# A two-layer streaming encoder step: attention, its entry and the kernel's end reworked together, and the engines' instruction order taken from a time line

## The chip, the cores and the metric

The kernel runs on one core of a Trainium2 chip. TensorE (PE in the profile) multiplies matrices, VectorE (DVE) and ScalarE (ACT) do elementwise work, GpSimd (POOL) does a little more of it, and SyncE (SP) issues most of the transfers. The metric is the device time of one execution in microseconds (us), taken as the median over several runs; lower is better.

## The reference

One step of a hybrid encoder over 1024 prompt rows and 64 sample rows (1088 columns in all, here stored transposed, features on the partitions). Layer 0 is a state-space mixer with a convolution, layer 1 a banded attention; a SwiGLU feed-forward network (FFN) follows each, and every sub-layer is wrapped in two RMSNorms.

```python
def rmsnorm(x, w):
    y = xf * lax.rsqrt(jnp.mean(xf * xf, axis=-1, keepdims=True) + EPS)
    return (y * w.astype(jnp.float32)).astype(x.dtype)

def swiglu(u, w_in, w_out):
    g, up = jnp.split(u @ w_in, 2, axis=-1)
    return (jax.nn.silu(g) * up) @ w_out

def shared_kv(x, kv_norm_w, w_kv):
    kv = (rmsnorm(x, kv_norm_w) @ w_kv).reshape(b, L, 2, ATT_HEADS, ATT_HEAD_DIM)

def band_attend(q, k, v, qpos, kpos, rel_bias):
    ...
    s = jnp.einsum('bqhd,bkhd->bhqk', q, k).astype(jnp.float32) * (ATT_HEAD_DIM ** -0.5) + bias
    s = jnp.where(valid, s, -jnp.inf)
    p = jax.nn.softmax(s, axis=-1).astype(v.dtype)
    return jnp.einsum('bhqk,bkhd->bqhd', p, v)
...
    xp = xp + rmsnorm(mp, nw[1])
    xp = xp + rmsnorm(swiglu(rmsnorm(xp, nw[2]), ffn_w_in[layer], ffn_w_out[layer]), nw[3])
```

Each query sees its own 64-row chunk and the eight before it. There are 16 heads of 64; the kernel handles them as 8 pairs `j`.

## The kernel before, in words

**Precision.** Every large product is made of three: a weight tile and an activation are each split into a rounded high part and a remainder, and `passes` (L407) multiplies high by high, high by low and low by high (L415 to L417). So every weight block of 128x1024 that arrives by DMA in a tile `raw` costs ACT a copy (L312, the high part `hl`) and DVE a subtraction (L313, the low part).

**Weights.** `Weights` is a planner with a fixed order: `plan` lists the blocks, `load` issues their DMAs, `plain` (L242) splits them. Blocks of the key, value and query projections carry a scale by row (`kscale`, the norm's weight): POOL multiplies the block by it in place first (L248), and then the split follows. `W.pri` gives the split a priority, `W.eng` another engine for the subtraction (POOL for the first three blocks).

**Order.** The columns come in three slices `s` of 384, 384 and 320. PE's order is written out by hand: the program issues PE's instructions exactly in program order, and a small clock `st.t` decides where the side tasks (`st.spawn`, `yield cost, delay, condition`) are put between the units of a projection. The constants `EP_W`, `ER_W`, `EQ_W`, `AT_W1` and so on are delays of that clock. The other engines' orders and the order of the DMA issues on SP are chosen when the program is built, by a list scheduler which follows program order shifted by `tc.high_priority(n)` (n instructions earlier).

**Stages.** Mixer (to about 660 us), its output projection and the first FFN (to about 1650), attention (to about 2200), its output projection and the second FFN (to the end). In the mixer `Conv` (L710) turns a projection's result into a tile `raw`, filters it into a tile `cvt` of which there is one, and applies Silu into the destination.

**The FFN's second half** (`back`, from L1388 on): for each slice eight output tiles, 66 matmuls each; `end(s)` then normalizes the slice, adds the residual and, in layer 0, splits the sum as the attention's input `u[s]` and forms the next norm's sum of squares. `rb_steps` (L482) is the norm's chain: `rstd` (matmuls with a column of ones, L448, then eight small DVE operations), a diagonal matrix `dg` on DVE (L467), one matmul that spreads it (L475) and an ACT copy to `rb`.

**Attention.** For each pair `j` and slice `s` the units K, Q and V are projected in that order; `evk`, `evq`, `evv` scale each result by `rba[s]` and split it. Q's low part is written twice, on both halves of the partitions, by DVE (L1540). `v_task` transposes V. `att_task(j, b)` handles a block of 128 query rows for both heads of the pair in three steps whose order is kept by `cur`: A, the scores (L1610, L1611) into one of two PSUM tiles `S` and the softmax on DVE and ACT (L1617 to L1626); B, the transposes of the probabilities into the same PSUM ring (`ptp`, L1638) and their copies `pT` (L1642); C, the product with V (L1661), after each block. At the entry the units of slice 2 are issued only once slice 2's norm is done; `build_o` reads the attention's result back from DRAM for the output projection.

Of the kernel before, what the change touches and what calls it, by code (L numbers as in the profile page):

```python
# [16 lines left out]
P = 128  # L17
# [31 lines left out]
EP_W, ER_W, EQ_W = (9.4, 9.4, 5.0), (8.9, 8.9, 4.5), (11.0, 11.0, 11.0)  # L49
# [4 lines left out]
LDP, ENP = 1500, (0, 0, 1500)  # L54
# [8 lines left out]
NB0 = 5  # L63

NACC = 3
BIG = 1e30
# [134 lines left out]
class Weights:  # L201
# [40 lines left out]
    def plain(self, it):  # L242
# [3 lines left out]
        if it.get("kscale") is not None:  # L246
            v3 = r.rearrange("p (k m) -> p k m", m=P)
            self.nc.gpsimd.tensor_tensor(v3, v3, it["kscale"].unsqueeze(2).to_broadcast([P, KD, P]), op=ALU.mult)  # L248
        self.part(it, "w", None, r[:, :n])
# [85 lines left out]
def hybrid_kernel(  # L335
# [4 lines left out]
    nc = tc.nc  # L340
    V, A, G, PE = nc.vector, nc.scalar, nc.gpsimd, nc.tensor
# [101 lines left out]
    def rstd(ssum, inv, r, nb, more=None):  # L443

        sp, ts = ax("nst"), [ssum] if more is None else [ssum, more]
        for i in range(nb):
            for j, t in enumerate(ts):
                PE.matmul(  # L448
                    sp[:, i:i + 1], t[:, i * P:(i + 1) * P], ones[:, 0:1], start=(j == 0), stop=(j == len(ts) - 1)
                )  # L450
        with tc.high_priority(HIP):
            v = nsb.tile([P, 12], F32, tag="nv", bufs=2, name="nv")
            a, h, y = v[:, 0:nb], v[:, 4:4 + nb], v[:, 8:8 + nb]
            V.tensor_scalar(a, sp[:, :nb], inv, EPS, op0=ALU.mult, op1=ALU.add)
            V.tensor_scalar(y.bitcast(I32), a.bitcast(I32), -0.5, float(0x5F3759DF), op0=ALU.mult, op1=ALU.add)
# [145 lines left out]
    with ExitStack() as es:  # L601
# [108 lines left out]
        class Conv:  # L710
# [5 lines left out]
            def __call__(self, s, ps_):  # L716
# [19 lines left out]
                cvt = sb2.tile([P, 384], F32, tag="cvt", bufs=1, name="cvt")  # L736
                cw = C_CW + ct * 4
                A.activation(cvt[:, :w_], raw[:, 0:w_], AF.Identity, bias=col(C_CB + ct), scale=col(cw))
                for k in range(1, 4):
                    V.scalar_tensor_tensor(  # L740
                        cvt[:, :w_], raw[:, k:k + w_], col(cw + k), cvt[:, :w_], op0=ALU.mult, op1=ALU.add
                    )
                if s < 2:
                    A.activation(dst[:, :384], cvt[:, :384], AF.Silu)
                else:
                    A.activation(dst[:, 0:256], cvt[:, :256], AF.Silu)  # L746
                    A.activation(dst[:, 256:320], cvt[:, 259:323], AF.Silu)
# [244 lines left out]
        W.eng = G  # L992
# [16 lines left out]
        for s in range(NSL):  # L1009
# [11 lines left out]
            for i in range(3):  # L1021
# [7 lines left out]
                if s == 2 and i == 2:  # L1029
                    W.eng = None  # L1030
# [245 lines left out]
    def back(layer, start, cpost, xsrc, xmid, cpre, cpost2, xout, rb_out, done2):  # L1276
# [3 lines left out]
        with ExitStack() as es:  # L1280
# [21 lines left out]
            def end_load(s):  # L1302
                o, n = SL[s]
                xc = Cells(n, (R, 99)) if s == 2 else Cells(n, (RX, 99), (R, 99))
                yield 0, EP_W[s], lambda: xc.room(KD)
# [5 lines left out]
            def end(s, y, ss, more=None):  # L1311
# [6 lines left out]
                yield from rb_steps(ss, n, out, ER_W[s], more=more)  # L1318
# [140 lines left out]
    for j in range(1, 8):  # L1459
        W.plan(W_K[j], W_Q[j], W_V[j])  # L1460
# [408 lines left out]
```

## Time and profile before

| what | us |
| --- | --- |
| median of 3 runs (lowest, highest) | 3090.92 (3090.6, 3097.8) |
| the profiled execution's own time | 3083.24 |
| its span, first to last instruction | 3081.1 |
| PE busy | 2989.6 |
| DVE busy | 2117.1 |
| ACT busy | 1419.9 |
| POOL busy | 880.4 |

The profile follows one execution. A row of a group gives engine, line, operation, written tile and read tiles, count and mean duration; a row of the timeline gives start and duration and, in brackets, how long the engine stood idle before it and which instruction ended that. "Granted clock" is the share of TensorE's full clock in a stretch. The profiled execution was 7.7 us faster than the median of the runs.

### The profile page before, as it was taken

How to read it: one execution, taken by the hardware profiler on the slowest of the kernel's cores; microseconds unless marked ns; L12 is line 12 of the kernel's file. 1: busy time of each engine (PE TensorE's matmuls, PEld its weight loads, DVE VectorE, ACT ScalarE, POOL GpSimd, SP SyncE). 2: the span in 40 equal slices, each digit the busy share in tenths (PEclk: the TensorE clock that was granted, in tenths of full speed). 3: DMA queues.
4: the chain of work that ended last, by engine and by line, in shares of the span. 5: the costliest groups of instructions: out<-in, count | busy, mean ns of one | idle time of the engine just before them, and what ended most of it. 6: DMA issues, size and time to landing. Idle time of an engine off the chain costs nothing.

```text
span 3081.1 us, 56781 instructions
## 1 busy us (share of the span) xinstructions
PE 2989.6 (97%) x21761; PEld 2908.2 (94%) x21761; DVE 2117.1 (69%) x4579; ACT 1419.9 (46%) x2512; POOL 880.4 (29%) x1011
## 2 busy tenths in 40 slices
PE   8999999999999999999999899999999999999998
PEld 8899999999999999999999788889898999999997
DVE  8878788796778545574566788887768645575544
ACT  6656565664443222344443454444554332244432
POOL 2333333331344343341223111100054334342112
PEclk9999999999999999999999999999999999999999
DMA  3111111125553222345663121122355222246654
GB/s 118 39 52 51 57 51 59 51 89 151 170 166 107 83 78 74 99 149 176 194 188 123 61 68 60 55 61 62 114 168 166 78 78 76 79 124 183 205 181 132
DMA packets 176511, 329.14 MB, mean 107 GB/s; under 512 B 17360, under 2 KB 124752, under 8 KB 176240
## 3 DMA queue, kind: packets, MB, share of 16 engines
q1 hardware_dynamic: 174448, 319.16, 33.4%
q0 software_dynamic: 1792, 6.36, 1.1%
q8 instruction: 171, 2.80, 0.4%
q14 instruction: 100, 0.82, 0.1%
HBM read 262.85 MB, written 62.60 MB: 106 GB/s over the span
## 4 chain that ended last, share of the span: by engine, by line
PE 81%; DVE 10%; DMA 3%; issue 2%; ACT 2%; POOL 2%; SPq 0%; DVEq 0%; POOLq 0%; ACTq 0%
PE mm L415 8%; PE px L1235 8%; PE px L1236 8%; PE px L1237 8%; PE mm L417 8%; PE mm L416 8%; PE po L1407 5%; PE po L1405 5%; PE po L1406 5%; PE mmx L415 2%; PE mmx L416 2%; PE mmx L417 2%; PE po L1661 2%; PE ptp L1638 2%; DVE hl L313 1%
## 5 line engine op out<-in xcount | busy, mean ns | idle before, releaser
L313 DVE TENSOR_TENSOR hl<-raw,hl 128x1024 fp32r<-128x1024 f32 (+1 forms) x292 | 359.7, 1233 | 313.5 <-ACT hl L312 312.9
L415 PE MATMUL mm<-r,hl 128*128 128x384 f32 (+2 forms) x1664 | 560.3, 337 | 5.9 <-ACT BT L746 4.8
L417 PE MATMUL mm<-r,hl 128*128 128x384 f32 (+2 forms) x1664 | 540.2, 325 | 0.6 <-DVE hl L313 0.6
L416 PE MATMUL mm<-r,hl 128*128 128x384 f32 (+2 forms) x1664 | 539.8, 324 | 0.0
L312 ACT CAST hl<-raw 128x1024 fp32r<-128x1024 f32 (+1 forms) x295 | 297.8, 1014 | 302.1 <-PE po L1407 98.7
L1236 PE MATMUL px<-r,hl 128*128 128x288 f32 (+1 forms) x1192 | 350.1, 294 | 0.0
L415 PEld LDWEIGHTS mm<-r,hl 128*128 128x128 f32 x1664 | 316.2, 190 | 14.6 <-issue 6.7
L441 POOL TENSOR_TENSOR ssum<-ssum,sq 128x256 f32<-128x256 f32 (+3 forms) x153 | 166.0, 1091 | 540.8 <-ACT sq L440 537.6
L416 PEld LDWEIGHTS mm<-r,hl 128*128 128x128 f32 x1664 | 316.5, 190 | 0.4
L417 PEld LDWEIGHTS mm<-r,hl 128*128 128x128 f32 x1664 | 315.6, 190 | 1.0 <-DVE hl L313 1.0
L1235 PE MATMUL px<-r,hl 128*128 128x288 f32 x1056 | 311.7, 295 | 4.1 <-DVE u L1250 3.9
L1237 PE MATMUL px<-r,hl 128*128 128x288 f32 x1056 | 311.2, 295 | 0.0
L1237 PE MATMUL px<-rx,hl 128*128 128x256 f32 x816 | 229.1, 281 | 6.5 <-DVE hl L313 6.5
L1235 PE MATMUL px<-rx,hl 128*128 128x256 f32 x816 | 230.0, 282 | 0.0
L1236 PEld LDWEIGHTS px<-r,hl 128*128 128x128 f32 x1192 | 224.0, 188 | 0.1
L1406 PE MATMUL po<-rx,hl 128*128 128x384 f32 (+1 forms) x640 | 208.0, 325 | 0.0
L1235 PEld LDWEIGHTS px<-r,hl 128*128 128x128 f32 x1056 | 198.7, 188 | 5.7 <-DVE u L1250 5.7
L1405 PE MATMUL po<-rx,hl 128*128 128x384 f32 (+1 forms) x608 | 199.6, 328 | 0.0
L1237 PEld LDWEIGHTS px<-r,hl 128*128 128x128 f32 x1056 | 198.4, 188 | 0.0
L1407 PE MATMUL po<-rx,hl 128*128 128x384 f32 (+1 forms) x608 | 198.0, 326 | 0.3 <-DVE hl L313 0.3
L1236 PE MATMUL px<-rx,hl 128*128 128x256 f32 x680 | 191.1, 281 | 0.0
L262 POOL TENSOR_TENSOR tt<-raw 128x512 f32<-128x512 f32 x44 | 60.0, 1363 | 396.9 <-DMA raw<-in_w_f_dram 207.8
(348 smaller groups left out, 8147.4 us busy)
## 6 DMA issues: line engine op xcount, KB each, us to landing
raw<-in_w_f_dram SPq DMA_DIRECT2D x204, 512.0 KB, 3.8
raw<-in_w_in_dram SPq DMA_DIRECT2D x40, 512.0 KB, 3.6
raw<-in_w_f_dram SPq DMA_DIRECT2D x48, 384.0 KB, 3.2
sg<-hscr SPq DMA_DIRECT2D x88, 192.0 KB, 3.6
raw<-in_w_so_dram SPq DMA_DIRECT2D x32, 512.0 KB, 3.9
raw<-in_w_kv_dram SPq DMA_DIRECT2D x18, 512.0 KB, 3.6
raw<-in_w_o_dram SPq DMA_DIRECT2D x16, 512.0 KB, 3.8
sg<-hscr SPq DMA_DIRECT2D x44, 160.0 KB, 3.6
```

Source lines behind the costliest of these rows:

```text
L312: self.nc.scalar.copy(h, v)
L313: (eng or self.eng or self.nc.vector).tensor_tensor(lo, v, h, op=ALU.subtract)
L415: PE.matmul(ps[:, :n], h_, xh, start=(first and i == 0), stop=False)
L416: PE.matmul(ps[:, :n], h_, xl, start=False, stop=False)
L417: PE.matmul(ps[:, :n], l_, xh, start=False, stop=(last and i == nk - 1))
L441: (eng or G).tensor_tensor(ssum[:, :n], ssum[:, :n], q[:, :n], op=ALU.add)
L1235: PE.matmul(ps, wh, ah[:, k, :], start=(k == 0), stop=False)
L1236: PE.matmul(ps, wh, al[:, k, :], start=False, stop=False)
L1237: PE.matmul(ps, wl, ah[:, k, :], start=False, stop=(k == 3))
L1405: PE.matmul(ps[:, :n], wh, xh, start=(k == 0), stop=False)
L1406: PE.matmul(ps[:, :n], wh, xl, start=False, stop=False)
L1407: PE.matmul(ps[:, :n], wl, xh, start=False, stop=(k == FT - 1))
```

## The change

- **Scheduler.** The whole kernel is traced in a second, inner context inside a critical section, with `schedule_with_timeline_sim=True`: the orders of DVE, ACT, POOL and SP come from another simulated machine. PE's order stays that of the program.
- **Weights with a row scale.** POOL's multiplication is gone; `scaled` makes the high part by eight ACT operations of 128x128 with a scale and the low part by eight DVE operations.
- **Mixer.** The convolution filters in place in its destination (`cvt` is gone); the first three weight blocks are subtracted by DVE, not POOL.
- **FFN's second half.** Weight splits get priority 1500 (`W.pri = LDP`). The end of slice 2 starts earlier (2.2 and 3.3 on the clock for 5.0 and 4.5), and its additions are all on DVE.
- **Entry.** Slice 2's K and V units of pair 0 are issued before slice 2's norm is done, and only their scaling waits for it; V of pair 1 for slices 0 and 1 comes before slice 2's Q.
- **Attention.** Order K, V, Q; score tasks are spawned by Q. The maximum's two small DVE operations go (the reduction runs on negated values and chains its start value). The second half of Q's low part is copied by a DMA on SP. Step C of a slice's three blocks is issued together, before step B of the next slice's first block. Scales at priority 3000, softmax and `pT` copies at 1000. Three tiles of Q become two, four of `pT` six. The last pair's result is taken from SBUF by `build_o`.
- **Kernel's end.** The last norm's two partial sums are summed in separate columns; six of the eight residual additions are made by PE (an identity times the residual, added in PSUM to an identity times the scaled result) and copied out by ACT.

```diff
-EP_W, ER_W, EQ_W = (9.4, 9.4, 5.0), (8.9, 8.9, 4.5), (11.0, 11.0, 11.0)
+EP_W, ER_W, EQ_W = (9.4, 9.4, 2.2), (8.9, 8.9, 3.3), (11.0, 11.0)
...
         if it.get("kscale") is not None:
-            v3 = r.rearrange("p (k m) -> p k m", m=P)
-            self.nc.gpsimd.tensor_tensor(v3, v3, it["kscale"].unsqueeze(2).to_broadcast([P, KD, P]), op=ALU.mult)
-        self.part(it, "w", None, r[:, :n])
+            self.scaled(it, r)
+        else:
+            self.part(it, "w", None, r[:, :n])
...
+    def scaled(self, it, r):
+
+        self.used.append(self.hl)
+        t = self.hl.get()
+        for k in range(KD):
+            sl, c = slice(k * P, (k + 1) * P), it["kscale"][:, k:k + 1]
+            self.nc.scalar.activation(t[:, 0, sl], r[:, sl], AF.Copy, scale=c)
+        for k in range(KD):
+            sl, c = slice(k * P, (k + 1) * P), it["kscale"][:, k:k + 1]
+            self.nc.vector.scalar_tensor_tensor(t[:, 1, sl], r[:, sl], c, t[:, 0, sl], op0=ALU.mult, op1=ALU.subtract)
+        it["w"] = t[:, 0, :], t[:, 1, :]
...
+    ctx.enter_context(tc.tile_critical())
+    tc = ctx.enter_context(tile.TileContext(nc, schedule_with_timeline_sim=True))
...
-        W.eng = G
...
             def end(s, y, ss, more=None):
...
+                    yield next(steps)
+                    hold(range(4))
+                    yield next(steps)
+                    yield next(steps)
+                    hold((4, 5))
+                    for m in range(KD):
+                        ym = y[:, m, :n]
+                        V.scalar_tensor_tensor(ym, ym, col(cpost2 + m), out[0], op0=ALU.mult, op1=ALU.mult)
+                        if m in xps:
+                            PE.matmul(xps[m][:, :n], ident, ym, start=False, stop=True)
+                            A.copy(ym, xps[m][:, :n])
+                        else:
+                            V.tensor_tensor(ym, ym, xs[m][0], op=ALU.add)
+                        nc.sync.dma_start(xout[:, m, o:o + n], ym)
...
-                yield 0, EQ_W[s]
+                yield (0, EQ_W[s]) if s < 2 else (0, 0, lambda: "k2" in done2)
...
             phase[0] = 2
+
+            W.pri = LDP
...
-                    for x in range(2):
-                        V.tensor_tensor(ql[H2[x], :n], qf[H2[e], :n], qh[H2[e], :n], op=ALU.subtract)
+                    V.tensor_tensor(ql[H2[e], :n], qf[H2[e], :n], qh[H2[e], :n], op=ALU.subtract)
+                    nc.sync.dma_start(ql[H2[1 - e], :n].bitcast(F32), ql[H2[e], :n].bitcast(F32))
+                for i in range(3):
+                    st.spawn(att_task(j, 3 * s + i), 5.0 + 0.1 * i)
...
-                if split < w_:
-                    V.tensor_tensor(mx[:L, 0:1], mx[:L, 0:1], mx[:L, 1:2], op=ALU.max)
-                V.tensor_scalar(mx[:L, 2:3], mx[:L, 0:1], -1.0, None, op0=ALU.mult)
-                A.activation(sc[:L, :w_], sc[:L, :w_], AF.Exp, bias=mx[:L, 2:3], accum_out=mx[:L, 3:4])
...
+                low = TOP
+                with tc.high_priority(ATP):
+                    for pi, (f0, f1) in enumerate([(0, split)] + ([(split, w_)] if split < w_ else [])):
+                        V.tensor_tensor_reduce(
+                            out=sc[:L, f0:f1], in0=sp[:L, pi, :f1 - f0], in1=brev[:, f0:f1],
+                            scale=-1.0, scalar=low, op0=ALU.add, op1=ALU.min, accum_out=mx[:L, pi:pi + 1],
+                        )
+                        low = mx[:L, pi:pi + 1]
...
+            cost = values(held) if i == 0 else 0
...
-        st.wait_for(lambda: ("rb", 2) in done)
...
-        for w, e in ((wk, evk), (wq, evq), (None, evv)):
-            units(w or W.get(), 0, e, (2,))
+        wv = W.get()
+        n2, kv2 = SL[2][1], []
+        for w in (wk, wv):
+            ps = mm("mm")
+            passes(ps, w, lambda k: u[2][k], [(k, k) for k in range(KD)], n2, parts=4)
+            kv2.append(ps)
+            done.append("k2")
+            st.pump()
+        st.wait_for(lambda: ("rb", 2) in done)
+        for ps, e in zip(kv2, (evk, evv)):
+            e(0)(2, ps)
             W.put()
+            st.pump()
```

More of the change, by code (lines that the diff above doesn't have):

```diff
@@ L1317, in end, with hold @@
                 out = []
-                yield from rb_steps(ss, n, out, ER_W[s], more=more)
+                if s == 2 and more is None:
+                    yield 0, EP_W[2]
+                steps = rb_steps(ss, n, out, ER_W[s], more=more)
+                if more is not None:
+                    xps = {}
+                    def hold(ms):
+                        for m in ms:
+                            xps[m] = mm("xp") if m > 3 else px.tile([P, 512], F32, tag="mm", name="xp")
+                            PE.matmul(xps[m][:, :n], ident, xs[m][0], start=True, stop=False)
+                    yield next(steps)
[12 more added lines that the diff above has]
+                        nc.sync.dma_start(xout[:, m, o:o + n], ym)
+                    for c in xs:
+                        xc.put(c)
+                    yr.put()
+                    return
+                yield from steps
                 for m in range(KD):
```

211 lines of the change are left out of this document (117 added, 94 removed).

## The prediction, made before the result was known

> **What bounds the kernel now.** The page first: how much of the span PE is busy, and who stands in the chain that ended last.
>
> ```profile
> span 3081.1 us, 56781 instructions
> PE 2989.6 (97%) x21761; PEld 2908.2 (94%) x21761; DVE 2117.1 (69%) x4579; ACT 1419.9 (46%) x2512; POOL 880.4 (29%) x1011
> PE 81%; DVE 10%; DMA 3%; issue 2%; ACT 2%; POOL 2%; SPq 0%; DVEq 0%; POOLq 0%; ACTq 0%
> ```
>
> PE is the bound, and the change takes no matmul away. All it can win is PE's idle time (3081.1 − 2989.6 = 91.5 us) and the slow clock behind a stall. So the next view is the busy time by stretches, cut at the stages that the change touches (stretch, length, then PE, PEld, DVE, ACT, POOL busy; granted clock).
>
> ```profile
> core 0: us, PE busy (x) PEld busy (x) DVE busy (x) ACT busy (x) POOL busy (x), PEclk, DMA share, GB/s
> 0.00:160.00 160.00, 144.77 (x933) 134.17 (x934) 132.44 (x327) 102.87 (x176) 44.69 (x96) 0.98 0.24 80
> 160.00:660.00 500.00, 499.35 (x3484) 484.54 (x3483) 399.75 (x1036) 305.36 (x478) 165.30 (x313) 1.00 0.17 54
> 660.00:1590.00 930.00, 919.43 (x6802) 911.48 (x6802) 590.63 (x1016) 380.58 (x663) 298.00 (x263) 1.00 0.44 134
> 1590.00:1610.00 20.00, 16.48 (x92) 15.95 (x91) 16.09 (x15) 10.28 (x19) 12.86 (x11) 0.83 0.64 201
> 1610.00:1670.00 60.00, 60.00 (x387) 59.54 (x387) 30.96 (x52) 22.43 (x37) 19.34 (x14) 1.00 0.42 129
> 1670.00:1700.00 30.00, 23.64 (x131) 22.83 (x130) 23.84 (x56) 13.49 (x29) 6.77 (x11) 0.83 0.36 118
> 1700.00:1800.00 100.00, 89.34 (x675) 80.15 (x674) 81.74 (x257) 48.51 (x110) 13.99 (x11) 0.97 0.19 58
> 1800.00:2200.00 400.00, 383.53 (x2984) 353.60 (x2984) 320.11 (x997) 195.32 (x434) 29.68 (x35) 1.00 0.21 63
> 2200.00:3000.00 800.00, 787.12 (x5849) 782.00 (x5848) 482.12 (x777) 318.77 (x538) 273.87 (x247) 0.99 0.45 135
> 3064.00:3081.10 17.10, 2.96 (x15) 1.85 (x14) 10.05 (x23) 0.86 (x2) 2.99 (x3) 0.60 0.22 77
> ```
>
> Idle on PE is length minus busy: 3.5 us at 1590, 6.4 at the entry (1670), 10.7 and 16.5 in attention, 14.1 at the end; 0.65 in 500 us of mixer, where nothing can be won and DVE is 80% busy. These five places are the ones that the change addresses.
>
> **The change part by part.**
>
> *Weights first in the FFN's second half.* PE's timeline around the stall, with two rows of the matmuls behind it:
>
> ```profile
> 1602.18 0.42 PE L1405 MATMUL po<-r,hl 128*128 128x320 f32 x1 [2.50 <-ACT hl L312]
> 1603.76 0.64 PE L1407 MATMUL po<-r,hl 128*128 128x320 f32 x1 [1.02 <-DVE hl L313]
> 1604.46 0.47 PE L1406 MATMUL po<-rx,hl 128*128 128x320 f32 x1
> 1609.53 0.47 PE L1407 MATMUL po<-rx,hl 128*128 128x320 f32 x1
> ```
>
> The weight's split stood behind the end of slice 1 on ACT and DVE. Between the last two rows 19 matmuls start, 0.267 us apart, where the stretch after has 60/387 = 0.155 on average: 20 x 0.11 = 2.2 us more. At priority 1500 against 0 the split goes first. Late next are slice 1's additions, by two splits (some 2.3 us), with 60 us until attention reads them. At most −5.7; I take −5. At the other end 0, if the block itself lands late.
>
> *Entry.*
>
> ```profile
> 1676.29 0.58 PE L448 MATMUL nst<-ones,ssum 128*128 128x1 f32 x2 [3.95 <-POOL ssum L1352]
> 1679.29 2.29 PE L448 MATMUL nst<-ones,ssum 128*128 128x1 f32 x10 [2.41 <-DVE ssum L1352]
> ```
>
> PE has only the norm of slice 2 left and waits 6.4 us for its sums. Now two units of 24 matmuls each (48 x 0.155 = 7.4 us) need no norm, the first ahead of these rows and the second between them and `nbp`; the end of slice 2 also starts 2.8 + 1.2 clock units earlier, and its eight additions no longer share the time with POOL (four more on DVE, about 2 us). Left is the wait from `rb` to the first free PSUM bank, about 1 us (copy and scale). I take −6; ends −7.4 and +4 (if the sums are as late as now and Q, moved behind V of pair 1, delays the first scores by that).
>
> *Attention.* First who PE waits for between 1690 and 2200, then the event that recurs once a pair: POOL's scaling of a weight block, DVE's Q remainders and PE's wait.
>
> ```profile
> PE ptp L1638 <- DVE mx L1617: 12.1, 7, 2.6
> PE S L1610 <- ACT pT L1642: 9.2, 10, 1.2
> L1540 DVE TENSOR_TENSOR Ql<-qf,Qh x52: 461/552/2228, 1847.7 to 2119.0; 64x384 fp32r<-64x384 f32 x32, 64x320 fp32r<-64x320 f32 x20
> 1848.66 3.10 DVE L1540 TENSOR_TENSOR Ql<-qf,Qh 64x320 fp32r<-64x320 f32 x3
> 1849.42 1.99 POOL L248 TENSOR_TENSOR raw<-raw,pcs 128x1024 f32<-128x1024 f32 x1 [2.04 <-DMA raw<-in_w_kv_dram]
> 1852.74 1.66 PE L1638 MATMUL ptp<-ident,sc 128*128 128x128 f32 x10 [1.47 <-DVE mx L1617]
> ```
>
> The two rows of waits hold 21.3 of the 27.2 us idle between 1700 and 2200: PSUM tiles that DVE or ACT had not emptied. At 1848.66 three remainders take 3.10 us where three of the shortest to the median (0.46 to 0.55) take 1.5: POOL runs from 1849.42 beside the last. Behind them the reductions come late, and the transposes wait for the tile until 1852.74.
>
> What DVE saves by pair: from 1850 to 2050 there are three pairs (48 negations on 128 partitions, 16 a pair: eight blocks of two heads), so a pair is about 67 us.
>
> ```profile
> L313 DVE TENSOR_TENSOR hl<-raw,hl 128x1024 fp32r<-128x1024 f32 x9 | 11.0, 1222 | 1.7 <-ACT hl L312 1.6
> L1623 DVE TENSOR_SCALAR mx<-mx 128x1 f32<-128x1 f32 x48 | 6.7, 150 | 0.5
> L1622 DVE TENSOR_TENSOR mx<-mx 128x1 f32<-128x1 f32 x24 | 3.7, 156 | 0.2
> 23.40 0.29 DVE L990 TENSOR_TENSOR dtw<-dtr,dtw 128x128 fp32r<-128x128 f32 x1
> 22.38 0.50 ACT L989 CAST dtw<-dtr 128x128 fp32r<-128x128 f32 x2
> L312 ACT CAST hl<-raw 128x1024 fp32r<-128x1024 f32 x9 | 9.4, 1048 | 11.3 <-issue 9.2 <-PE mm L417 1.9
> ```
>
> Half of twelve remainders (6 x 0.55 = 3.3), the negation and maximum ((6.7 + 3.7)/3 = 3.5) and one blocked stretch (1.6) go: 8.4 us of 320.11/6 = 53.4. Eight operations of 128x128 at most 8 x 0.29 = 2.3 replace a subtraction of about 1.2: 1.1 a block, 3.3 for three. Net −5 on DVE; ACT gets 8 x 0.25 − 1.05 = 1 more per block, with half its time free. POOL loses 1.99 a block and stands ahead of no split any more. Higher priority on softmax and `pT` empties PSUM sooner. What stays: V's products of three blocks now stand in one piece, and a slice's first transposes stand behind them.
> I take −16, some 0.6 of the idle time. Ends: −27, and +23 for one wait as the row of 1.47 at each of 24 slices less the 12.1 gone.
>
> *Q's remainder by DMA.* Not shown before; the nearest transfers of its size:
>
> ```profile
> out_kT_dram<-kf SPq DMA_DIRECT2D x3, 128.0 KB, 1.7
> SPq L1669 <- ACT ot L1668: 105.8, 22, 18.3
> ```
>
> So 1.7 us (64 x 384 x 4 = 96 KB), against 0.55 on DVE, and behind whatever SP's queue waits for: `ot` was waited for up to 18.3 us. Cover: Q is projected one slice (a third of a pair, 22 us) ahead of its scores. I take 0; uncovered it costs 1.7 − 0.55 = 1.2 for each of 24 slices, 28 us.
>
> *End.*
>
> ```profile
> 3068.16 1.43 PE L475 MATMUL nbp<-dg,frac 128*128 128x320 f32 x2 [2.23 <-DVE dg L467]
> 1659.85 0.70 PE L475 MATMUL nbp<-dg,frac 128*128 128x320 f32 x2
> 3070.09 4.30 DVE L1326 SCALAR_TENSOR_TENSOR y<-y,pcs,rb 128x320 f32<-128x320 f32 x5 [1.98 <-ACT rb L479]
> 3075.24 2.08 DVE L1327 TENSOR_TENSOR y<-y,r 128x320 f32<-128x320 f32 x5
> 3077.25 0.54 DVE L1324 SCALAR_TENSOR_TENSOR y<-y,pcs,r 128x320 f32<-128x320 f32 x1
> ```
>
> From `rb` to the end of DVE's last, 3077.8, is 7.7 us; the scalings take 4.30/5 = 0.86 each while POOL works on three of the eight. After: eight at 0.54 and two additions at 2.08/5 = 0.42, 5.2 in all. PE's last six identities at 0.70 (4.2) and ACT's copies run beside. The four held ones (2.8) fill the 2.23 idle ahead of `nbp` and 0.6 more; `nbp` then takes 0.70 for 1.43. So −2.5 + 0.6 − 0.7 = −2.6. Cold, at 1.43 each, the four would take 5.7 (+3.5 ahead of `nbp`) and the six 8.6, 0.9 over the 7.7 of now, and a last copy of 0.4: about +5. The Trainium skill ("TensorE: Matmul & The Clock Gate", section "What's actually happening") says that the clock halves after an idle window of about 3.4 us and is whole again after as long a busy one. By that rule a tail of short bursts could stay cold, and the sum would be 7.6 worse; the pair 1.43 and 0.70 agrees with the halving, though the idle time before it was 2.23 only.
>
> *The rest.* The in-place filter and three subtractions moved from POOL to DVE: 0, between −3.6 and +3.6 (3 x 1.2 on a DVE that is 83% busy in the first 160 us). Entering and leaving an inner context: +1, between 0 and 2.1 (what lies around the span now, 3083.24 − 3081.1, once more). A new order for four engines everywhere else: 0; it can win at most the idle of the untouched stretches (15.2 + 0.65 + 10.6 + 12.9 = 39), and its loss is a rival.
>
> Sum: −5 − 6 − 16 − 2.6 + 1 = −28.6, so 3054.6 for an execution like the profiled one. That one was 7.7 under the median; on the median's scale 3090.9 − 28.6 = 3062.
>
> **The rivals.** 0.3% (9 us) is about what a measurement can tell from no change here.
>
> *The gain is eaten in attention.* Q's DMA is uncovered (28 us), because SP's queue holds it or Q comes late; or the merged products make PE wait as often as now. Against it the 22 us of lead. From 17 slices on (17 x 1.2 = 20) what is left is under 9 us. Time 3091 − 29 + 28 = 3090.
>
> *Slower: the new order costs the mixer.* PE has no idle time there only because order and hand-written delays fit.
>
> ```profile
> L821 ACT ACT_TABLE_LOAD x38 | 48.8, 1283 | 32.7 <-DVE dm L817 32.4
> ```
>
> Of 160 to 660 us this is one place of loads; Exp and Silu alternate in each step, and every further split of an Exp pair adds 1.283 us to the chain from `bcp` to the product. With 48 steps (16 pairs of heads by 3 slices), one load more on each: 48 x 1.283 = 62 us, so 3062 + 62 = 3124. It decides from 23 uncovered loads on (29/1.283). For it: DVE at 80%; against: ACT has 39% of the stretch free, and each of its 38 steps has 500/38 = 13 us. The Trainium skill ("ScalarE: Activation LUTs", "What ACT_TABLE_LOAD costs") gives 2.66 us for a switch with its drain; by that estimate it would be 128 us, but the row shows 1.283 and no drain.
>
> *The tail stays cold:* −28.6 + 7.6 = −21, 3070; for it the 1.43 of now, against it that the held identities leave no gap. *The order helps everywhere:* half of the 39 us besides: about 3042.
>
> **How the numbers follow.** Forecast 0.55, of which 0.12 with a cold tail (own range 3045 to 3078); helps everywhere 0.06, eaten 0.12, slower 0.27. So faster 0.61, same 0.12, slower 0.27. The range goes from 3036 to 3116: it leaves out some 0.03 below and the worse half of the slower case, 0.15, above.
>
> **What would show it.** No wait over 1 us at the second FFN slice's weights near 1600; PE busy through the entry; waits of `ptp` on the reduction down from 12.1 to under 4 in all, and Q remainders of 0.5 only; the tail after the last FFN matmul at 14 us for 17. Mixer idle above 10 us, or more than 38 table loads at the line of the Exp there, would make it wrong.

## The result and the profile after

The changed kernel takes 3110.68 us (3104.76 to 3114.58) against 3090.92 us of the kernel before: a ratio of 1.0057, 95% interval 1.0041 to 1.0072. It is slower, by about 18 us (20 between the medians), where 29 us faster was forecast. It lies inside the range (3036 to 3116), in the case that had 0.27.

The page of the changed kernel, its span and its busy times:

```profile
span 3109.1 us, 57030 instructions
PE 3000.5 (97%) x21785; PEld 2927.8 (94%) x21785; DVE 2066.3 (66%) x4498; ACT 1455.8 (47%) x2701; POOL 817.7 (26%) x975
```

DVE has 51 us less to do (2117.1 before) and POOL 63 us less, as the change says. PE has more of both: 108.6 us idle for 91.5, and 3000.5 us busy for 2989.6 with only 24 matmuls added. PE's waits (what it waited for, us in all, times, longest) say where:

```profile
PE nbp L490 <- DVE dg L482: 13.1, 6, 4.0
PE po L1445 <- DVE hl L313: 12.8, 10, 2.6
PE nst L463 <- POOL ssum L455: 10.3, 5, 3.8
...
PE px L1247 <- DVE p L1264: 5.9, 2, 3.1
...
PE ptp L1688 <- DVE mx L1666: 2.2, 3, 1.1
```

The wait that led the list before, of the transposes for the reduction (12.1 us), is down to 2.2. New at the top are waits for the norm's chain (`dg`, the diagonal matrix, and `ssum`, its sums), for the sums `p` of the FFN's first half, and for weight splits. Two rows of the kernel before for the same work: `dg` 2.2 us once, and 2.3 us in all for the splits of the FFN's second half:

```profile
PE po L1407 <- DVE hl L313: 2.3, 4, 1.0
PE nbp L475 <- DVE dg L467: 2.2, 1, 2.2
```

Three of these waits on PE's timeline of the changed kernel, with what follows the third:

```profile
825.72 1.19 PE L490 MATMUL nbp<-dg,frac 128*128 128x256 f32 x2 [3.02 <-DVE dg L482]
...
998.63 0.39 PE L1247 MATMUL px<-rx,half 128*128 128x256 f32 x1 [3.09 <-DVE p L1264]
...
1641.01 0.60 PE L1445 MATMUL po<-rx,hl 128*128 128x320 f32 x1 [2.54 <-DVE hl L313]
1641.41 0.47 PE L1443 MATMUL po<-rx,hl 128*128 128x320 f32 x1
...
1644.35 0.38 PE L1445 MATMUL po<-rx,hl 128*128 128x320 f32 x1
1644.57 0.31 PE L1443 MATMUL po<-rx,hl 128*128 128x320 f32 x1
```

A wait is paid more than once: for 3.3 us behind the third the matmuls take 0.47 us each for 0.31, and start 0.267 us apart for 0.147 later. Twelve of them cost 12 x 0.12 = 1.4 us on top of the 2.54. So waits make PE's busy time grow too. The same 21785 matmuls in the list order (`e2_rework_inner_plain`, below) keep PE busy for 2985.1 us, at a mean granted clock of 0.992 for 0.985 here:

```profile
PE 2985.1 (98%) x21785; PEld 2915.1 (95%) x21785; DVE 2074.0 (68%) x4498; ACT 1461.0 (48%) x2703; POOL 814.9 (27%) x975
```

The Trainium skill ("TensorE: Matmul & The Clock Gate", section "What's actually happening") has the clock halve after an idle window of about 3.4 us and recover after as long a busy one; the 3.3 us agree, but here 2.54 us of waiting were enough.

### The profile page after: what moved, and what is told of

It reads as the page before. It is cut to its first block, busy times and chain, and to the rows that moved or that the text cites. A ratio compares the mean times of both kernels' runs of the same rounds, so it can differ in the third digit from the quotient of the medians.

```text
span 3109.1 us, 57030 instructions
## 1 busy us (share of the span) xinstructions
PE 3000.5 (97%) x21785; PEld 2927.8 (94%) x21785; DVE 2066.3 (66%) x4498; ACT 1455.8 (47%) x2701; POOL 817.7 (26%) x975
## 5 line engine op out<-in xcount | busy, mean ns | idle before, releaser
L313 DVE TENSOR_TENSOR hl<-raw,hl 128x1024 fp32r<-128x1024 f32 (+1 forms) x269 | 321.7, 1197 | 305.3 <-ACT hl L312 303.5
L312 ACT CAST hl<-raw 128x1024 fp32r<-128x1024 f32 (+1 forms) x269 | 271.5, 1010 | 290.1 <-DMA raw<-in_w_f_dram 120.6
```

What stands on the lines that cost most here:

```text
L312: self.nc.scalar.copy(h, v)
L313: (eng or self.eng or self.nc.vector).tensor_tensor(lo, v, h, op=ALU.subtract)
```

## The experiments

### The three parts apart: the rework, the inner context, the time line

The change holds three things: the rework of the kernel, an inner context in a critical section, and in it the order from the time line. Two runs take parts off the changed kernel.

`e1_rework_plain_order`: the rework alone, in the outer context.

```diff
-    ctx.enter_context(tc.tile_critical())
-    tc = ctx.enter_context(tile.TileContext(nc, schedule_with_timeline_sim=True))
+
+
```

> The changed kernel without the inner context and its time line: the rework alone, the engines' order chosen as in the kernel before. Theory A (the order costs the time, the rework wins it): the forecast's sum holds, 3091 - 30 = 3061 us, faster by 0.7 to 1.2%; the first FFN's pairs begin at about 952 us as before (981 in the changed kernel), the last score at about 2177. Theory B (the rework itself costs outside attention: in-place filter, subtractions on DVE, weight splits first): the start of the pairs stays at about 980 and the time at 3105 to 3115. Theory C (both by halves): about 3085.

`e2_rework_inner_plain`: the inner context stays, the order is that of the list scheduler.

```diff
-    tc = ctx.enter_context(tile.TileContext(nc, schedule_with_timeline_sim=True))
+    tc = ctx.enter_context(tile.TileContext(nc, schedule_with_timeline_sim=False))
```

> The changed kernel with the inner context kept and the time line switched off. Theory A with the time line as the cause: within 3 us of the run without an inner context, 3061 to 3065 (the context costs one entry and one exit, 0 to 2 us). Rival: the inner context itself is what changes the order for the worse; then about 3110 as in the changed kernel.

`e3_before_time_line` and `e4_before_inner_plain`: the kernel before with the same two lines added, with `True` and with `False`.

> The kernel before with the inner context and the time line, and nothing else of the change. Theory A: it pays what the order costs without what the rework wins, 3091 + 48 = 3139 (3125 to 3150), with the pairs of the first FFN starting near 981. Theory B: the order is harmless, 3085 to 3095, pairs near 952.

> The kernel before in an inner context without the time line. Theory A: 3091 to 3094, the cost of entry and exit alone. Rival (the inner context disturbs the order): over 3100, and then the time line's own part is the difference to the run of the kernel before with the time line.

Measured, as ratios to the kernel before (3087.0 us on that chip), with 95% intervals:

| order | kernel before | rework |
| --- | --- | --- |
| outer context, list order | 1 | 0.9849 (0.9832 to 0.9866), 3038.6 us |
| inner context, list order | 1.0049 (1.0032 to 1.0065), 3101.0 us | 0.9919 (0.9902 to 0.9935), 3060.7 us |
| inner context, time line | 1.0184 (1.0164 to 1.0205), 3140.9 us | 1.0057 (1.0041 to 1.0072), the change |

So the rework alone is worth 1.5%, some 47 us, more than the 29 forecast for everything. The inner context costs 15 us on one kernel and 22 on the other (0.0049 and 0.0070 of 3087). The time line's order costs 42 and 43 us (0.0135 and 0.0138): the same on both, so it is no matter of the rework. A difference of two ratios, here and below, is uncertain by some 7 us either way (two intervals of 0.0017).

Against what was expected: the rework alone is on the side of Theory A (the pairs of the first FFN start at 958.2 us, not at 980), but 22 us faster than its figure of 3061. `e2` meets its 3061 to 3065 almost to the microsecond, and by luck: its condition, within 3 us of the run without the inner context, fails by 19. `e3` is Theory A (3140.9 for 3139, the pairs at 979.8). `e4` lies above 3100, as its rival had it, but not for the rival's reason: its trace has every engine's instructions in the same order as in the kernel before.

PE's hand-written order and its delays were the same in all of these runs. Whether another order on PE would suit the time line's orders better was not run.

Where each part acts can be read from landmarks, the starts of the same work in each profile (us; from the views of one tile's instructions, which give the first and last start of each group):

| | before | + inner | + time line | rework | + inner | + time line |
| --- | --- | --- | --- | --- | --- | --- |
| first transposes of the mixer | 91.4 | 96.0 | 91.2 | 98.2 | 102.6 | 89.3 |
| last transposes of the mixer | 657.4 | 663.1 | 663.3 | 664.1 | 669.1 | 663.8 |
| FFN 1, first half, first matmul | 951.8 | 960.1 | 979.8 | 958.2 | 965.7 | 980.5 |
| FFN 1, second half, first matmul | 1372.5 | 1382.1 | 1408.0 | 1378.6 | 1388.7 | 1406.8 |
| attention, first scores | 1694.0 | 1704.6 | 1740.5 | 1686.9 | 1700.7 | 1723.1 |
| attention, last scores | 2206.1 | 2215.6 | 2245.7 | 2167.2 | 2184.1 | 2220.5 |
| FFN 2, second half, last matmul | 3063.8 | 3078.1 | 3127.3 | 3023.3 | 3042.5 | 3093.2 |
| end | 3081.1 | 3097.7 | 3146.4 | 3037.0 | 3058.4 | 3109.1 |

The last column less the one before it: the time line wins 13 us at the start, has given back 8 of them by the end of the mixer, is 15 us behind at the first FFN, 22 at the first scores, 36 at the last, and 51 at the end. So the largest losses are the 20 us between the mixer and the first FFN (its output projection and the norms), 14 in attention and 14 behind it; the long first half of the first FFN loses only 3. (The columns are of one execution each. The 51 us at the end, where the ratios give 43, are of executions in different rounds, in which the kernel before took 3090.9 and 3087.0 us.)

PE's order is the same in these two kernels and every engine has the same instructions (but for 2 of ACT's 100 table loads), so what differs is the order on the other engines and what comes late for it. DVE's timeline in the changed kernel, ahead of two of the waits shown above:

```profile
820.22 0.16 DVE L478 SCALAR_TENSOR_TENSOR nr<-nv 128x2 f32<-128x2 f32 x1
820.29 0.46 DVE L577 TENSOR_TENSOR r<-sg,r 128x288 fp32r<-128x288 f32 x1
820.66 3.03 DVE L1180 SCALAR_TENSOR_TENSOR rx<-rx,pcs,rb 128x256 f32<-128x256 f32 x5
823.61 0.45 DVE L577 TENSOR_TENSOR r<-sg,r 128x288 fp32r<-128x288 f32 x1
823.98 1.26 DVE L1180 SCALAR_TENSOR_TENSOR rx<-rx,pcs,rb 128x256 f32<-128x256 f32 x3
825.16 0.41 DVE L482 TENSOR_TENSOR dg<-ident,nr 128x256 f32<-128x256 f32 x1
...
993.43 0.41 DVE L1262 TENSOR_TENSOR u<-px,p 128x256 f32<-128x256 f32 x1
993.76 3.88 DVE L1122 TENSOR_TENSOR r<-r 128x1152 fp32r<-128x1152 f32 x3
997.57 0.68 DVE L281 TENSOR_TENSOR tt<-raw,tt 128x512 f32<-128x512 f32 x1
998.17 0.41 DVE L1264 TENSOR_TENSOR p<-px,p 128x256 f32<-128x256 f32 x1
```

And the same two places with the list order (`e2_rework_inner_plain`):

```profile
816.68 0.15 DVE L478 SCALAR_TENSOR_TENSOR nr<-nv 128x2 f32<-128x2 f32 x1
816.76 0.46 DVE L577 TENSOR_TENSOR r<-sg,r 128x288 fp32r<-128x288 f32 x1
817.13 0.42 DVE L482 TENSOR_TENSOR dg<-ident,nr 128x256 f32<-128x256 f32 x1
...
976.00 0.41 DVE L1262 TENSOR_TENSOR u<-px,p 128x256 f32<-128x256 f32 x1
976.33 1.68 DVE L280 TENSOR_TENSOR tt<-tt,raw 128x512 f32<-128x512 f32 x1
977.93 1.35 DVE L1122 TENSOR_TENSOR r<-r 128x1152 fp32r<-128x1152 f32 x1
979.20 0.41 DVE L1264 TENSOR_TENSOR p<-px,p 128x256 f32<-128x256 f32 x1
```

The diagonal matrix needs `nr` and nothing else. In the list order it starts 0.5 us behind `nr`; in the time line's, eight scalings and two subtractions stand between, and it is 4.9 us. At the second place 4.6 us of work that has time stand ahead of `p`, for 3.0 in the list order. There `u`, just ahead, was late as well: PE waits 1.88 us for it at 993.9. In these rows DVE works in the order that it was given, so an urgent operation that is put behind a long one waits, however ready it is.

### Is an urgent chain that loses its place enough?

The rows show it, but no run so far made that change alone. `e13_chains_without_priority` does, in the plain order: the priority 3000 is taken from the norm's chain, its diagonal matrix, its copy to `rb`, and from the sums of the FFN's first half, `u` and `p` among them.

```diff
-        with tc.high_priority(HIP):
+        with tc.high_priority(0):
             v = nsb.tile([P, 12], F32, tag="nv", bufs=2, name="nv")
...
-        with tc.high_priority(HIP):
+        with tc.high_priority(0):
             dg = diag(nr[:, :nb], nb)
...
-        with tc.high_priority(HIP):
+        with tc.high_priority(0):
             out.append(bcast(dg, 0, n, rb))
...
-            with tc.high_priority(HIP):
+            with tc.high_priority(0):
                 if p_ == P1:
```

> The rework in the plain order, with the priority 3000 taken from the norm's chain (the small operations, the diagonal matrix, the copy to rb) and from the sums u and p, and nothing else changed. Between the rework's inner plain order and its time line, with the same instructions and the same order on PE, PE's waits for the diagonal matrix go from under 1 to 13.1 us and for p from under 1 to 5.9 us, and 43 us are lost. Theory A, an urgent chain that other DVE work gets into is enough to lose time: 10 to 30 us slower than the rework in the plain order, ratio 0.988 to 0.995, with waits for the diagonal matrix and for u and p of 2 to 4 us each at several norms. Theory B, the waits named are only where delays from elsewhere (late weights, late transfers) show: ratio 0.984 to 0.987, and these waits stay as they were.

Ratio 0.9982 (0.9972 to 0.9991), 3080.3 us: 41 us slower than the rework in the plain order, more than Theory A gave. PE's waits in it, and one of them with what stands ahead of it on DVE:

```profile
PE px L1247 <- DVE u L1262: 17.5, 4, 8.8
PE nbp L490 <- DVE dg L482: 13.5, 5, 5.7
```

```profile
987.00 6.42 DVE L1122 TENSOR_TENSOR r<-r 128x1152 fp32r<-128x1152 f32 x5
993.34 0.41 DVE L1262 TENSOR_TENSOR u<-px,p 128x256 f32<-128x256 f32 x1
```

```profile
993.81 0.58 PE L1247 MATMUL px<-rx,hl 128*128 128x256 f32 x1 [7.85 <-DVE u L1262]
```

The waits stand at the same places as in the changed kernel (at 830, 994, 1724, 2299 and 2394 us here; 826, 994 and 999, 1739, 2309 and 2413 there). So losing the place of these chains is enough to lose as much as the time line loses. It isn't shown that it is all of it, and PE's waits say that it is about half. Here PE idles 28.6 us more than in the plain order, and 27 of them are waits for these chains. In the changed kernel PE idles 35 us more than in `e2` (108.6 for 73.3), and these chains have some 18 of them; weight splits of the FFN's second half have 8.4, sums on POOL 6.5, and the inputs of the mixer's transposes 6.4. No run takes these others away.

### What the inner context costs

The list order inside and outside of the inner context is the same, instruction by instruction and wait by wait, but for a few branches and barriers at both ends. The difference of 22 us is in how long things take. SyncE's timeline of the rework in the outer and then in the inner context (start, duration of the issue):

```profile
1101.00 0.33 SPq L224 DMA_DIRECT2D raw<-in_w_f_dram  x1
```

```profile
1101.58 0.50 SPq L224 DMA_DIRECT2D raw<-in_w_f_dram  x1
```

and the median from issue to landing of the same transfers, in the same order:

```profile
raw<-in_w_f_dram SPq DMA_DIRECT2D x204, 512.0 KB, 3.6
```

```profile
raw<-in_w_f_dram SPq DMA_DIRECT2D x204, 512.0 KB, 4.0
```

Each issue takes 0.17 us longer (0.33 and 0.50 are the medians of all 1119 issues on SyncE too), and these transfers land 0.4 us later; the kernel before shows the same (0.33 and 3.8 against 0.50 and 4.0). Everything that goes through a transfer is a little later; PE's waits for `u` rise from 4.8 to 6.6 us, and the granted clock of the first 100 us falls from 0.93 to 0.90. The time is not lost evenly but in steps: the same matmul starts 4.9 us later at any point of the mixer from 205 to 664 us, 8.0 later from 1031 to 1280 in the first half of the first FFN, and 17.9 from 2434 to 2684 in that of the second. So a stream of matmuls that waits for nothing runs as fast as before. Of the 21.4 us between the two spans (3037.0 and 3058.4) 9.7 are idle time of PE, and 11.7 are busy time at a lower granted clock (0.995 and 0.992). No run changes the issues alone, so that they are the whole cause is argued, not shown.

`e8_small_section_first` asks whether it is enough to stand behind such a section:

```diff
+    with tc.tile_critical(), tile.TileContext(nc) as tn, tn.tile_pool(name="first", bufs=1) as fp:
+        nc.vector.memset(fp.tile([P, 4], F32, name="first"), 0.0)
```

> The rework in the plain order, with a critical section and an inner context ahead of it that hold one small memset; the kernel itself stays in the outer context, and each engine's order is that of the plain one. The rework wholly inside an inner context has the same instructions in the same order, and yet its DMA issues take 0.45 to 0.50 us on SP for 0.33, its transfers land 0.2 to 0.4 us later, and it is 22 us slower. Theory A, it is enough that the code stands behind the section's branch: issues of 0.45 to 0.50 and ratio 0.990 to 0.993. Theory B, it takes being inside the section (or the size of the section): issues of 0.33, ratio 0.985 to 0.987 with 2 to 5 us of entry and exit.

Ratio 0.9853 (0.9839 to 0.9868), and issues of 0.33 us: Theory B. Entering and leaving a section costs 1 us by these ratios, uncertain by some 7, in line with what I had put; being in it makes each issue dearer. What it is about the section that does this, its size or something else, stays open.

### What the parts of the rework are worth

All in the plain order; the reference is the ratio 0.9849 of `e1_rework_plain_order`, and 0.001 is 3.1 us. In its profile the same matmuls stand 6.8 us later than in the kernel before from 90 us on, 6.0 at 1565, 2.2 at 1645, 41 us earlier at 2250, 39.7 at 2810, and 44 at the end. So it loses 7 us at the start, wins 4 in the FFN's second half, 43 in the entry and attention, and 4 at the end. PE's waits in it that answer to those of attention before (12.1 and 9.2 us):

```profile
PE S L1656 <- DVE pT L1693: 4.8, 11, 0.8
...
PE ptp L1688 <- DVE mx L1666: 2.6, 7, 0.7
```

*The startup.* `e5_startup_as_before` undoes both edits there; `e11_first_weights_by_pool` only the second:

```diff
+                cvt = sb2.tile([P, 384], F32, tag="cvt", bufs=1, name="cvt")
...
+        W.eng = G
         first = [("B", 0), ("C", 0), ("x", 0)]
...
+                if s == 2 and i == 2:
+                    W.eng = None
```

> The rework in the plain order, with the two edits of the startup undone (the first three weight blocks subtracted by POOL again, the filter into its own tile again). In the plain-order rework the first transposes of the mixer start at 98.2 us, in the kernel before at 91.4, and from there to 1590 us the distance stays at 6 to 7 us. Theory A, the two edits cost this: ratio 0.9849 - 0.0022 = 0.983 (about 3032 us), first transposes at 91 to 92 us. Theory B, the edits are worth nothing, as I had put them, and the 7 us come from the other parts that act there (the split with a scale, the norm's columns): ratio 0.985, first transposes at 98.

> The rework in the plain order, with the first three weight blocks subtracted by POOL again and the filter left in place. Undoing both had the mixer 4.5 us earlier. If the subtractions are the cost: the same 4.5 us at 240 us into the span, ratio 0.9835 +- 0.0015. If the filter's own tile was what gave it: 0 to 1 us, ratio 0.985.

Ratios 0.9844 (0.9829 to 0.9859) and 0.9840 (0.9824 to 0.9855; 3033.6 us). The times don't separate them from each other or from the reference. In the profiles the mixer's work stands 4.5 and 4.1 us earlier than in the reference at 240 us, and still 2.9 and 6.1 earlier at 2960. So the subtractions moved from POOL to DVE cost 4 of the 7 us; the filter's own tile nothing that can be seen. That is Theory A of `e5` for the most part (first transposes at 92.4 us, for 91 to 92) and the first case of `e11`, though only the profiles show it. Where the other 2 to 3 us come from stays open. `e11` has the lowest median of all, though the intervals don't set it apart.

*Q's low part.* `e6_q_low_by_dve` subtracts both halves on DVE:

```diff
-                    V.tensor_tensor(ql[H2[e], :n], qf[H2[e], :n], qh[H2[e], :n], op=ALU.subtract)
-                    nc.sync.dma_start(ql[H2[1 - e], :n].bitcast(F32), ql[H2[e], :n].bitcast(F32))
+                    for x in range(2):
+                        V.tensor_tensor(ql[H2[x], :n], qf[H2[e], :n], qh[H2[e], :n], op=ALU.subtract)
```

> The rework in the plain order, with both halves of Q's low part subtracted by DVE again and no DMA. If the DMA is covered and DVE's time in attention is what was won (24 slices of two remainders, 48 x 0.55 = 26 us more DVE in a stretch of 480 us that has 100 free): ratio 0.986 to 0.988, 3 to 10 us slower than 0.985. If the DMA was late for the scores and cost what it saved: ratio 0.983 to 0.985. If DVE is not what attention waits for: 0.985 within 0.002.

Ratio 0.9884 (0.9867 to 0.9900), 11 us slower, just past the 3 to 10 expected: the transfer is covered, and DVE's time is worth something. DVE is busy 2097.8 us for 2075.5, so 22 us of DVE are worth 11. In the plain-order rework the copies land after some 2 us, and PE waits for none of them.

*The scaling.* `e7_scale_by_pool` multiplies the weight block on POOL ahead of the split:

```diff
-            self.scaled(it, r)
-        else:
-            self.part(it, "w", None, r[:, :n])
+            v3 = r.rearrange("p (k m) -> p k m", m=P)
+            self.nc.gpsimd.tensor_tensor(v3, v3, it["kscale"].unsqueeze(2).to_broadcast([P, KD, P]), op=ALU.mult)
+        self.part(it, "w", None, r[:, :n])
```

> The rework in the plain order, with the row scale multiplied by POOL in place ahead of the split again. Attention won 43 us where I had put 16 and the entry 6. Theory A, POOL's multiplication beside DVE is the larger part of what held attention (24 blocks of 2 us, each stopping DVE): ratio 0.990 to 0.995, 15 to 30 us slower, and remainders of 2 us again in the profile. Theory B, the new order of the steps (values of three blocks in one piece, K and V ahead of Q, priorities) is what won: ratio 0.985 to 0.988, under 10 us slower.

Ratio 0.9888 (0.9871 to 0.9905), 12 us slower: between the two theories, though the remainders of 2 us, Theory A's sign, are back. The remainders of Q on DVE (shortest, median, longest ns), in this run and then in the changed kernel:

```profile
L1583 DVE TENSOR_TENSOR Ql<-qf,Qh x48: 464/552/2103, 1674.2 to 2156.0; 64x384 fp32r<-64x384 f32 x32, 64x320 fp32r<-64x320 f32 x16
```

```profile
L1583 DVE TENSOR_TENSOR Ql<-qf,Qh x48: 473/548/558, 1709.6 to 2194.6; 64x384 fp32r<-64x384 f32 x32, 64x320 fp32r<-64x320 f32 x16
```

Beside POOL's multiplication an operation of 0.55 us takes up to 2.1; without it none is over 0.56.

*Priorities and the maximum.* `e9_priorities_as_before` and `e10_maximum_as_before`:

```diff
-LDP, ENP, ATP = 1500, (0, 0, 1500), 1000
+LDP, ENP, ATP = 1500, (0, 0, 1500), 0
...
-                with tc.high_priority(HIP):
+                with tc.high_priority(0 if j else HIP):
                     V.scalar_tensor_tensor(qf[:, :n], p_[:, :n], 0.125, rba[s][:, :n], op0=ALU.mult, op1=ALU.mult)
```

(likewise for V; for K the priority ends with the second pair), and

```diff
-                            scale=-1.0, scalar=low, op0=ALU.add, op1=ALU.min, accum_out=mx[:L, pi:pi + 1],
+                            scale=1.0, scalar=0.0, op0=ALU.add, op1=ALU.max, accum_out=mx[:L, pi:pi + 1],
...
+                    if split < w_:
+                        V.tensor_tensor(mx[:L, 0:1], mx[:L, 0:1], mx[:L, 1:2], op=ALU.max)
+                    V.tensor_scalar(mx[:L, 2:3], mx[:L, 0:1], -1.0, None, op0=ALU.mult)
```

> The rework in the plain order, with attention's priorities as they were before (softmax and copies of the probabilities at 0, the scales of K, Q and V at 0 from the third and the second pair on). Undone alone, Q's DMA was worth 11 us and the scaling moved off POOL 12, of 43 that the entry and attention won. Theory A, the priorities carry most of the remaining 20: ratio 0.990 to 0.993, and PE's waits for the reduction and for the probabilities' copies rise from 7.4 us to over 15. Theory B, the plain list order had these instructions early enough: 0.984 to 0.987.

> The rework in the plain order, with the maximum and the negation as two small DVE operations again: 72 blocks of two heads each, 96 to 144 negations and half as many maxima of 0.15 us, 25 to 35 us more of DVE between 1690 and 2180 us. By the price that Q's DMA showed (26 us of DVE for 11 us of time): 10 to 14 us slower, ratio 0.988 to 0.990. If they fill time in which DVE has nothing ready: 0.985 to 0.986.

Ratios 0.9895 (0.9878 to 0.9913) and 0.9863 (0.9845 to 0.9881): the priorities are worth 14 us, the maximum 4, the latter not separated from nothing. For the priorities that is the lower edge of Theory A, and its waits came too: 2.2 us for the reduction and 13.6 for the copies.

For the maximum I had expected 10 to 14, by adding up durations. The 224 small operations are there, and their durations add up to 33.6 us, but they overlap with their neighbours: DVE is busy 2084.9 us for 2075.5, only 9.4 more. By busy time the price agrees with that of Q's low part (4 us for 9.4 and 11 for 22), within the uncertainty of both. So an engine's load is read from its busy time, not from a sum of durations.

*The merged product with V.* `e12_values_by_block`:

```diff
-            cost = values(held) if i == 0 else 0
+            cost = values(held)
```

(with the wait for V's transposes at every block, for the first of three only.)

> The rework in the plain order, with each block's product with V issued ahead of the next block's transposes, not three blocks' in one piece. Theory A, the merged piece gives DVE and ACT time to empty PSUM and is a large part of the 20 us left: ratio 0.989 to 0.993, with PE's waits for the reduction and the copies over 15 us. Theory B, finer pieces fill PE's waits better: 0.981 to 0.984. If it doesn't matter: 0.985.

Ratio 1.0097 (1.0082 to 1.0113), 77 us slower, far outside every theory, and the reason isn't the one given. PE's longest wait in it, then DVE, ACT and SyncE ahead of it:

```profile
1915.36 0.69 PE L1688 MATMUL ptp<-ident,sc 128*128 128x128 f32 x2 [8.14 <-DVE mx L1666]
```

```profile
1914.02 0.69 DVE L1527 TENSOR_TENSOR Ck<-cr,Ck 64x512 fp32r<-64x512 f32 x1 [7.38 <-ACT Ck L1526]
1914.74 0.56 DVE L1666 CUSTOM_DVE_ANT_0 sc<-S,bias 128x384 f32<-128x384 f32 x1
```

```profile
1913.37 1.26 ACT L1526 CAST Ck<-cr 64x512 fp32r<-64x512 f32 x2 [8.02 <-DMA cr<-in_ckT_dram]
```

```profile
1906.13 2.53 SPq L224 DMA_DIRECT2D raw<-in_w_kv_dram  x1
1908.75 1.13 SPq L1524 DMA_DIRECT2D cr<-in_ckT_dram  x2
```

The reduction isn't late because DVE is busy. It is queued on DVE behind the split of the next pair's cached keys, which ACT can't copy before their transfer has landed, and that was issued behind two weight blocks (the second is the row at 1906.13). ACT waits 46 us for these transfers in this run and 7.4 in the reference. These waits are what the run prices, an early split of late data on engines that work in order, and it says nothing on the merged piece itself: that the pieces' order and the loading of `Ck` hang together is shown, what merging alone is worth isn't.

Undone one at a time, the four parts cost 11, 12, 14 and 4 us, 41 in all of the 43 that the entry and attention won. With some 7 us of uncertainty on each, that they add up so well is chance; they needn't, and the new order of the steps may hold some of it.

## Why the prediction was wrong

The forecast summed the edits and took the two lines about the scheduler as nearly free. Both of those steps failed.

*"A new order for four engines everywhere else: 0."* This is the step that decided the sign: it costs 42 to 43 us on either kernel. The loss did have a rival, with 0.27, but at the wrong place. I looked for it in the mixer, by more table loads, and the rows of the changed kernel say no (the busy times by stretches, and the loads there):

```profile
160.00:660.00 500.00, 496.10 (x3457) 480.64 (x3456) 392.25 (x1027) 298.05 (x468) 163.60 (x310) 1.00 0.17 53
```

```profile
L836 ACT ACT_TABLE_LOAD x38 | 48.8, 1283 | 63.9 <-DVE dm L832 63.9
```

Idle rose from 0.65 to 3.9 us, and the 38 loads are the same (98 in the whole kernel, for 100). The mixer did lose some time to the time line, 8 us between its first and last transposes, but not to loads. I had bounded the gain of a new order by the idle time of the untouched stretches (39 us), and should have bounded its loss likewise: by the chains that are short, urgent and off PE, and that the list order keeps together. `e13` shows that in the plain order these alone hold 41 us; in the changed kernel about half of PE's added waiting is theirs. That the sign fell into the 0.27 case is luck: neither the place nor the mechanism was the one given there.

*"Entering and leaving an inner context: +1, between 0 and 2.1."* Measured 15 and 22 us. The bound was taken from what lies around the span, and `e8` is in line with that much; but the cost is inside, with 0.17 us more on every issue, which nothing in the trace of before could show. It ought to have stood as an unknown with a wide upper end.

*"Entry −6" and "Attention −16."* Mis-sized: 43 us in the plain order. The mechanisms were right (12.1 us of waits for the reduction became 2.6, and the remainders no longer take 2.2). I took 0.6 of PE's idle time, and left out that fewer waits also shorten the busy time behind them: PE is busy 2973.4 us in the plain rework for 2989.6, at a mean granted clock of 0.995 for 0.990. The priorities, to which I gave a sentence and no number, are worth 14. In the changed kernel the entry isn't filled. PE waits 4.01 us for `dg`, as the norm's chain on DVE there is interleaved with weight splits and softmax:

```profile
1738.63 1.41 PE L490 MATMUL nbp<-dg,frac 128*128 128x320 f32 x2 [4.01 <-DVE dg L482]
```

*"Q's remainder by DMA: 0"*, with a rival that the transfer would eat everything (28 us). Undoing it costs 11 us, and PE waits for no such copy in the plain-order rework, so the rival was wrong and the cover is there.

*"Weights first in the FFN's second half: −5."* 3.8 us in the plain order (6.0 late before it, 2.2 behind it), close. In the changed kernel the stall is still there: the row at 1641.01 with 2.54 us. DVE's timeline ahead of it:

```profile
1635.70 3.59 DVE L1383 TENSOR_TENSOR r<-y,r 128x384 fp32r<-128x384 f32 x4
1639.21 1.75 DVE L313 TENSOR_TENSOR hl<-raw,hl 128x768 fp32r<-128x768 f32 x1
```

ACT's copy of the block, which the split needs, ends at 1636.02; the split starts 3.2 us later, behind four subtractions of slice 1, the very thing that the priority was to prevent.

*"End −2.6."* From the last FFN matmul to the end it is 17.3 us before, 13.7 in the plain rework, 15.9 in the changed kernel: right in kind, −3.6 and −1.4. The tail isn't cold in the plain order:

```profile
3020.00:3037.00 17.00, 12.61 (x63) 9.44 (x61) 7.11 (x21) 3.41 (x8) 0.00 (x0) 0.99 0.23 77
```

*"The in-place filter and three subtractions: 0, between −3.6 and +3.6."* In the plain order the mixer starts 6.8 us late. Undoing both edits gives back 4.5 of them at 240 us, outside the bounds, and 4 are the subtractions, on a DVE that I had noted to be 83% busy there; the rest belongs to no term of the sum. In the changed kernel the time line's order more than hides it (first transposes at 89.3 for 91.4).

Of the signs that I had named, the waits of `ptp` and the remainders came true, the stall at 1600 and the filled entry didn't, the tail half did, and the mixer's idle time and loads, which were to tell if I was wrong, stayed quiet while the kernel got slower: they watched a stage that holds 8 of the 51 us lost.

## What to carry to other kernels

Measure a change of scheduler or context apart from the edits that come with it: here edits worth 47 us were hidden by two lines that cost 65. Where one engine is the bound at 97%, the order of the others matters at the few short chains that it waits for, and here a simulated time line that put longer work into them lost 42 us or so on both kernels. An instruction placed early on data that come late holds up everything behind it on its engine (8.0 us at one transfer in `e12`), so look at what an engine was waiting for, not only at how busy it is.

## What the runs showed of the hardware that was not expected

Inside a critical section with an inner context the same DMA issue on SyncE takes 0.50 us for 0.33, and the same 512 KB land after 4.0 us for 3.6, with every engine's order unchanged (`e1` and `e2`); after a section that has ended the issue takes 0.33 again (`e8`). The Trainium skill ("DMA: Bandwidth & Descriptors", section "Anatomy of one DMA — SWDGE (gpsimd) path") puts about 50 ns of a transfer's fixed cost on the sequencer's dispatch, for another kind of queue than this one; on SyncE's queue the rows show 330 to 500 ns.
